# Wide products and transfer-made sums in the first up projection of a decoder trunk, with the down projection's kept sums put earlier

## The chip, the cores and the metric

The kernel runs on one core of a Trainium2 chip. The metric is the time of one execution on the device in microseconds (us); the shown time is the median of three runs. TensorE (PE) multiplies, VectorE (DVE) and ScalarE (ACT) work on tiles, GpSimd (POOL) and SyncE (SP) issue transfers. Transfers that SP or ACT issue go through the hardware queues q1 and q10, those that POOL issues through the software queue q0. All of them are carried by the same 16 DMA engines.

## The reference

One layer over 512 positions of width 1024: two half-weighted SwiGLU blocks around a token mixer, then a last norm. Everything is float32.

```python
def swiglu(x, w_gate, w_up, w_down):
    return (jax.nn.silu(x @ w_gate) * (x @ w_up)) @ w_down
...
        x = x + 0.5 * swiglu(rmsnorm(x, ffn1_norm[l]), ffn1_wg[l], ffn1_wu[l], ffn1_wd[l])
        x = x + hybrid_mixer(rmsnorm(x, mix_norm[l]), w_in[l], conv_w[l], conv_b[l],
...
        x = x + 0.5 * swiglu(rmsnorm(x, ffn2_norm[l]), ffn2_wg[l], ffn2_wu[l], ffn2_wd[l])
    return rmsnorm(x, final_norm)
```

The change touches the first SwiGLU only: its up projection (`w_gate` and `w_up` together, 2816 columns each, 22 tiles of 128 for gate and for up) and the sums of blocks of `w_down` that its down projection will use.

## The kernel before

**Precision.** Every product of two float32 matrices is made of three matmuls on pairs of a high part h and a rest l: h times yh, l times yh, h times yl. ACT copies a weight tile to its high part (`wh`), and DVE subtracts (`wl`).

**The start.** SP issues the eight tiles of x (256 KB each) mixed with three weight tiles in chunks of 128 KB (`wr`), then four more weight tiles of 512 KB (`ahead`), all on q1; ACT issues three small transfers on q10. PE multiplies the three weight tiles as the x tiles come. The first of the four `ahead` tiles (`AH[0]`) is split by `given` (ACT `wh<-ahead`, DVE `wl<-ahead`) and gives the fourth product, `gemm(pu, w, y, range(KD))`.

**The plain tiles.** `ffn_up` begins with eight plain ("direct") tiles of 24 matmuls of 512 columns, in the loop over `d`. At this time SP has no more than the next raw tiles to load.

**The stream.** Then come 16 units w of a block scheme, seven block products each where plain multiplication has eight; per unit the order is 1, 2, 4 (of the unit before), 6, 3 (of the unit before), 5, 7. Product p of unit w multiplies a sum of weight blocks by a sum of activation blocks: s1, s3 are formed by POOL transfers with accumulation into SBUF, s2 = s1 + a11 and s4 = s2 + a12 by DVE in `add_weights`. A narrow product has 12 matmuls of 256 columns into one half of a PSUM tile. A wide one has 4 of 512 columns (h with both halves of the moving operand, into both halves of the tile) and 4 of 256 columns, and its two halves are then added by DVE. Products 2, 5 and 3 are wide (`WIDE`). `step(i)` emits, behind product i, the reading of product i-1 (`results`) and the preparation of the weights of product i+4 (`prepare`). An activation function put into the list `functions` is emitted one step later.

**The down projection's sums.** `block_down` keeps a table of tasks. Task number n is emitted when `ahead(i - len(stream))` reaches n, so with 112 products in the stream, task -90 comes in step 22. For each of eight column blocks j, a sum `kept` in DRAM is made by two POOL transfers of 256 KB: a plain one DRAM to DRAM (task 5j - 90, line 891) and an accumulating one (task 5j - 83, line 892). They are read only in the down projection (`fetch_sum`).

**Order.** Inside `tc.manual_schedule(engines=ENGINES)` the order on each engine is the order of the code. An instruction waits for the semaphores of what it needs. POOL has nothing but its transfers here.

Of the kernel before, what the change touches and what calls it, by code (L numbers as in the profile page):

```python
# [176 lines left out]
def hybrid_kernel(ctx, tc, xt, vec, w1u, w1d, wm, wki, wrg, watt, wrnn, wout, w2u, w2d, gf, out):  # L177
# [224 lines left out]
    class W:  # L402
        pass

    WIDE = (2, 5, 3)

    def weight_blocks(wu, n0, first):

# [7 lines left out]
    def ffn_up(y, wu, n0, hs, g, waiting=(), given=(), ahead=None, blocks={}, wide=()):  # L416
# [10 lines left out]
        ws = [W() for _ in range(count)]  # L427
        for w, o in enumerate(ws):
            o.j, o.blocks = w % 2, blocks.get(w)
            o.wide = range(1, 8) if o.blocks else wide  # L430
        loaded, pairs = [0], {}

        direct = [(n, j) for n in range(n0, f0) for j in range(2)]
# [39 lines left out]
        def load():  # L473

            w = loaded[0]
            loaded[0] += 1
            o = ws[w]
            n = f0 + w // 2 * 2
            u, v = wu[n, o.j], wu[n + 1, o.j]
            if blocks and w + 2 >= min(blocks):  # L480
                o.x = slot(F32, "a11"), slot(F32, "a12")
                for b in range(2):
                    Q.dma_start(o.x[b], u[:, b * H:(b + 1) * H])
            else:
                x_ = raw.tile([P, WMAX], F32, tag="raw", name=nm("wr"))
                o.x = x_[:, :H], x_[:, H:]
                Q.dma_start(x_, u)
            o.s1, o.s3, o.a22 = (slot(F32, t) for t in ("s1", "s3", "a22"))
            Q.dma_start(o.s1, v[:, :H])
            Q.dma_start(o.s3, v[:, :H])  # L490
            Q.dma_start(o.a22, v[:, H:])
            yield
            G.dma_start(o.s1, v[:, H:], accum_op=ALU.add)
            G.dma_start(o.s3, u[:, :H], accum_op=ALU.add)
# [9 lines left out]
        def add_weights(i):  # L504
            p, w = stream[i] if i < len(stream) else (0, 0)
            o = ws[w]
            if o.blocks:
                return
            if p == 6:
                o.s2 = slot(F32, "s2")  # L510
                V.tensor_add(o.s2, o.s1, o.x[0])
            if p == 3:
                o.s4 = slot(F32, "s4")
                V.tensor_add(o.s4, o.s2, o.x[1])

# [13 lines left out]
        def prepare(i):  # L529
            if i < LEAD:  # L530
                add_weights(i)
            if i + 1 >= LEAD:
                add_weights(i + 1)
            p, w = stream[i]
            o = ws[w]
            even = i // 2 * 2
            if i % 2 == 0:
                units.append([wsp.tile([P, WMAX], F32R, tag=t, name=nm(t)) for t in ("wh", "wl")])
            if formed(even) and formed(even + 1):
                if i % 2 == 0:  # L540
                    wsplit(pairs.pop(i // 2), *units[-1])
                    fetch_pair(i + 2 * RAWS)
                return
            h, l = (t[:, i % 2 * H:(i % 2 + 1) * H] for t in units[i // 2])
            if formed(i):
                wsplit(pairs[i // 2][:, i % 2 * H:(i % 2 + 1) * H], h, l)
            else:
                wsplit({1: lambda: o.x[0], 2: lambda: o.x[1], 6: lambda: o.s2, 5: lambda: o.s1, 7: lambda: o.s3,
                        4: lambda: o.a22, 3: lambda: o.s4}[p](), h, l)
            if i % 2:  # L550
                fetch_pair(even + 2 * RAWS)

# [24 lines left out]

        def function(t, o):
            if o.wide:
                functions.append(t)  # L580
            else:
                A.activation(t, t, AF.Silu)

# [3 lines left out]
        def results(p, o, first):  # L587
            if p == 1:
                o.t1, o.t2 = (work("tg"), work("tg")) if o.j == 0 else (awork("tu"), awork("tu"))
                A.activation(o.t1[:, lo], o.beta[:, lo], AF.Copy)  # L590
            elif p == 2:
                V.tensor_sub(o.t1[:, lo], o.p2[:, lo], o.t1[:, lo])
                if p in o.wide:
                    V.tensor_add(o.t1[:, lo], o.t1[:, lo], o.p2[:, hi])
            elif p == 6:
                A.activation(o.t1[:, hi], o.beta[:, lo], AF.Copy)
            elif p == 7:
                A.activation(o.t2[:, hi], o.beta[:, lo], AF.Copy)
                V.tensor_add(o.t2[:, hi], o.gamma[:, lo], o.t2[:, hi])
                if 5 in o.wide:  # L600
                    V.tensor_add(o.t2[:, hi], o.t2[:, hi], o.gamma[:, hi])
                if o.j:
                    o.h2 = slot(F32, "h")
                    V.tensor_mul(o.h2[:, hi], o.t2[:, hi], first.t2[:, hi])
                else:
                    function(o.t2[:, hi], o)
            elif p == 4:
                if o.j:
                    V.tensor_mul(o.h2[:, lo], o.beta[:, lo], first.t2[:, lo])
                else:  # L610
                    A.activation(o.t2[:, lo], o.beta[:, lo], AF.Silu)
            elif p == 3:
                V.scalar_tensor_tensor(o.t1[:, hi], o.gamma[:, lo], -1.0, o.t1[:, hi], op0=ALU.mult, op1=ALU.subtract)
                if p in o.wide:
                    V.tensor_sub(o.t1[:, hi], o.t1[:, hi], o.gamma[:, hi])
                if o.j:
                    o.h1 = slot(F32, "h")
                    V.tensor_mul(o.h1, o.t1, first.t1)
                    hs.extend((o.h1, o.h2))
                else:  # L620
                    function(o.t1, o)
# [43 lines left out]
        def step(i):  # L665


            ready = functions[:]
            functions.clear()
            p, w = stream[i - 1] if i else (0, 0)  # L670
            o, first = ws[w], ws[w - 1]
            if p and o.blocks:
                copies(p, o)
                if p in (2, 3):
                    reads(p, o, first)
            elif p:
                results(p, o, first)
            if i + LEAD < len(stream):
                prepare(i + LEAD)
            if p and o.blocks and p not in (2, 3):  # L680
                reads(p, o, first)
            for t in ready:
                A.activation(t, t, AF.Silu)

        with tc.manual_schedule(engines=ENGINES):
            for _ in range(len(raws), RAWS + len(raws)):
# [2 lines left out]
            operands, norm = moving_operands(g), norm_steps(acc)  # L689
            for d, (n, j) in enumerate(direct):  # L690
                sums.append(psum(("aux", "mm")[n % 2]))
                if d == 1:
                    norm_rest(norm)
                    hs.extend(ffn_act(*p) for p in waiting)
# [58 lines left out]
    def block_down(hs, wd, sums, blocks=None):  # L753
# [100 lines left out]
        for i, st in enumerate(steps):  # L854
# [33 lines left out]
                task(3 * j // 2 + 4, add)  # L888
            if p == 7:
                kept = scr.tile([P, S], F32, name=nm("scr"))  # L890
                task(5 * j - 90, lambda j=j, o=kept: nc.gpsimd.dma_start(o, block(2, j)))
                task(5 * j - 83, lambda j=j, o=kept: nc.gpsimd.dma_start(o, block(0, j), accum_op=ALU.add))

                def fetch_sum(j=j, o=kept):
                    s3[j] = slot(F32, "s3")
# [95 lines left out]

    sums = []
    d1 = block_down(hs, w1d, sums)
    ffn_up(y, w1u, 2, hs, V_G1, ((WP[0], WP[1]), (WP[2], pu)), AH[1:], d1.tasks_at, wide=WIDE)

    BLOCKS2D = down_blocks(w2d)
    BLOCKS2U = weight_blocks(w2u, 0, UNITS)
# [1011 lines left out]
```

## Time and profile before

| | us |
|---|---|
| median of three runs (1065.58 to 1066.42) | 1065.99 |
| the profiled execution | 1064.61 |
| its span, first to last instruction | 1062.8 |
| PE busy | 1052.4 (99%) |
| DVE busy | 881.4 (83%) |
| ACT busy | 667.0 (63%) |
| POOL busy | 235.0 (22%) |

All durations below are from the profiled execution, whose time is 1.8 us over its span and 1.4 us under the median. Times in a timeline count from the start of the span. "PEclk" is the granted clock of TensorE as a share of its higher level, "DMA share" the mean busy share of the 16 DMA engines. A matmul's row gives its own time from first to last column; successive matmuls overlap, so what a product takes is read from start to start.

### The profile page before, as it was taken

The page shows a single profiled execution, that of the slowest core. Times are in us where ns is not written, and L with a number is a line of the kernel's source. Part 1 is how long each engine was busy: PE and PEld are TensorE (multiplying, and loading weights), DVE is VectorE, ACT ScalarE, POOL GpSimd, SP SyncE. Part 2 cuts the span into 40 slices and gives each one's busy share as a digit, 9 for nine tenths or more (in the row PEclk, how much of TensorE's full clock was granted, in tenths as well). Part 3 has the DMA queues.
Part 4 walks back from the last instruction along what each step waited for, and adds up shares of the span by engine and source line. Part 5 has one row for each costly group of instructions (what it writes and reads, how often), then busy time and mean ns, then how long its engine had stood idle before and what let it go on. Part 6 is the DMA issues. An engine that isn't in the chain of part 4 may idle for free.

```text
span 1062.8 us, 16803 instructions
## 1 busy us (share of the span) xinstructions
PE 1052.4 (99%) x5812; PEld 914.6 (86%) x5812; DVE 881.4 (83%) x1730; ACT 667.0 (63%) x1250; POOL 235.0 (22%) x357
## 2 busy tenths in 40 slices
PE   9999999999999999999999999999999999999997
PEld 7889999989999788888888888888899888888885
DVE  6688888889988879998899867766888888888875
ACT  6565656655576657976886664446656666565663
POOL 0161241102131021212031444442643000000020
PEclk9999999999999999999999999999999999999999
DMA  7398899638794487667594878995997666545573
GB/s 279 73 253 203 212 256 235 163 112 247 173 225 120 127 221 183 171 181 184 135 227 129 215 170 201 268 243 151 250 280 182 200 196 194 183 146 170 188 204 121
DMA packets 93973, 203.71 MB, mean 192 GB/s; under 512 B 11712, under 2 KB 20032, under 8 KB 93248
## 3 DMA queue, kind: packets, MB, share of 16 engines
q1 hardware_dynamic: 60144, 136.24, 39.0%
q0 software_dynamic: 33024, 65.55, 31.9%
q8 instruction: 46, 0.75, 0.3%
q10 hardware_dynamic: 720, 0.84, 0.2%
q14 instruction: 39, 0.32, 0.1%
HBM read 191.58 MB, written 48.23 MB: 226 GB/s over the span
## 4 chain that ended last, share of the span: by engine, by line
PE 90%; DVE 6%; ACT 2%; issue 1%; DMA 1%; ACTq 0%; DVEq 0%
PE mm L171 63%; PE aux L171 27%; DVE wl L171 2%; ACT wh L171 1%; DVE am L171 1%; DVE ca L171 1%; ACT cm L171 1%; DMA wr<-wm 0%; DVE xc L171 0%; DVE h L171 0%; DMA vt<-vec 0%; DVE cb L171 0%; DVE tu L171 0%; DVE tg L171 0%; DVE cm L171 0%
## 5 line engine op out<-in xcount | busy, mean ns | idle before, releaser
L171 DVE TENSOR_TENSOR wl<-wr,wh 128x1024 fp32r<-128x1024 f32 (+2 forms) x241 | 237.8, 990 | 72.3 <-ACT wh L171 70.1
L171 ACT ACTIVATE wh<-wr 128x1024 fp32r<-128x1024 f32 (+3 forms) x243 | 208.4, 864 | 75.6 <-issue 23.6
L171 PE MATMUL mm<-cm,wh 128*128 128x256 f32 (+1 forms) x1280 | 250.4, 300 | 0.0
L171 PEld LDWEIGHTS mm<-cm,wh 128*128 128x128 f32 x1280 | 202.8, 191 | 5.1
L171 PE MATMUL mm<-cm,wl 128*128 128x256 f32 x736 | 184.5, 282 | 0.0
L171 PE MATMUL mm<-yh,wh 128*128 128x512 f32 (+1 forms) x416 | 163.7, 394 | 0.4 <-ACT wh L171 0.2
L171 PE MATMUL mm<-yl,wh 128*128 128x512 f32 (+1 forms) x416 | 162.3, 390 | 0.0
L171 PE MATMUL mm<-yh,wl 128*128 128x512 f32 x408 | 159.3, 390 | 0.0
L171 PEld LDWEIGHTS mm<-cm,wl 128*128 128x128 f32 x736 | 133.7, 191 | 4.1
L171 PE MATMUL aux<-cm,wh 128*128 128x512 f32 (+1 forms) x472 | 123.4, 380 | 0.8 <-ACT cm L171 0.5
L171 PEld LDWEIGHTS mm<-yh,wh 128*128 128x128 f32 (+1 forms) x416 | 78.0, 187 | 17.2 <-ACT i L171 0.6
L171 PEld LDWEIGHTS mm<-yl,wh 128*128 128x128 f32 (+1 forms) x416 | 77.6, 187 | 15.6 <-DVE yl L171 0.5
L171 PEld LDWEIGHTS mm<-yh,wl 128*128 128x128 f32 x408 | 76.6, 188 | 16.3
L171 PEld LDWEIGHTS aux<-cm,wh 128*128 128x128 f32 x472 | 79.8, 190 | 10.8 <-ACT cm L171 0.9
L171 ACT ACTIVATE wh<-s 128x512 fp32r<-128x512 f32 x96 | 59.8, 626 | 41.9 <-DVE s L171 38.4
L171 PEld LDWEIGHTS aux<-cm,wl 128*128 128x128 f32 x440 | 68.7, 189 | 8.6
L171 PE MATMUL aux<-cm,wl 128*128 128x256 f32 x440 | 73.9, 281 | 0.0
L171 DVE TENSOR_TENSOR wl<-s,wh 128x512 fp32r<-128x512 f32 x96 | 64.8, 686 | 5.4 <-ACT wh L171 5.3
L325 POOL DMA_DIRECT2D scr<-w2d x32 | 29.8, 1050 | 174.7 <-DMA scr<-w2d 149.3
L159 POOL DMA_DIRECT2D cm<-h x16 | 13.7, 865 | 205.8 <-ACT cm L171 197.1
L171 PE MATMUL mm<-wh,cm 128*128 128x512 f32 x192 | 59.1, 389 | 0.0
L1010 POOL COPY beat<-beat 128x1 f32<-128x1 f32 x67 | 25.0, 373 | 126.7 <-DVE beat L1009 117.1
(263 smaller groups left out, 2138.3 us busy)
## 6 DMA issues: line engine op xcount, KB each, us to landing
wr<-scr SPq DMA_DIRECT2D x80, 256.0 KB, 3.0
wr<-wm SPq DMA_DIRECT2D x39, 512.0 KB, 4.3
scr<-w2u POOLq DMA_DIRECT2D x72, 256.0 KB, 5.7
wr<-w1u SPq DMA_DIRECT2D x21, 512.0 KB, 5.1
scr<-scr POOLq DMA_DIRECT2D x40, 256.0 KB, 5.3
wr<-w1d SPq DMA_DIRECT2D x18, 512.0 KB, 4.4
wr<-w2u SPq DMA_DIRECT2D x36, 256.0 KB, 3.0
wr<-w2d SPq DMA_DIRECT2D x36, 256.0 KB, 3.0
```

The source lines that it names most:

```text
L159: return self.engine.dma_start(out, src, **kw)
L171: return call(*args, **kw)
L325: plain, adds = nc.gpsimd.dma_start, lambda o, i: nc.gpsimd.dma_start(o, i, accum_op=ALU.add)
L1010: nc.gpsimd.tensor_copy(paces[-1], paces[-1])
```

## The change

It has three parts.

1. **Width.** In the first up projection, units 4 to 15 get `WIDE1`, so products 1 and 6 are wide as well. For product 1, ACT copies 512 instead of 256 columns to a tile `c`, DVE subtracts over 512 columns and `joined` adds the halves. For product 6, ACT copies the upper half out of PSUM, DVE adds the lower half to it in PSUM (`o.beta[:, lo]`), and ACT copies the sum out again; in units 4 to 14 that last copy goes through `functions`, one step later.
2. **s4.** In these 12 units s4 is made by an accumulating POOL transfer of a12 (256 KB from DRAM) into the tile of s2, behind the splitting of s2.
3. **Kept sums.** The 16 transfers of the eight kept sums move to tasks j//4 - 200 and j//4 - 199, and the loop over the plain tiles calls `ahead(d - 200)`.

```diff
-    WIDE = (2, 5, 3)
+    WIDE, WIDE1 = (2, 5, 3), (1, 2, 6, 5, 3)
...
-            o.wide = range(1, 8) if o.blocks else wide
+            o.wide = range(1, 8) if o.blocks else wide if w >= 4 or not wide else WIDE
...
-            if p == 3:
+            if p == 3 and 6 not in o.wide:
                 o.s4 = slot(F32, "s4")
                 V.tensor_add(o.s4, o.s2, o.x[1])
...
+            if p == 6 and 6 in o.wide and not o.blocks:
+                o.s4 = o.s2
+                G.dma_start(o.s4, o.a12, accum_op=ALU.add)
...
-                A.activation(o.t1[:, lo], o.beta[:, lo], AF.Copy)
+                if p in o.wide:
+                    o.c = slot(F32, "c")
+                    A.activation(o.c, o.beta, AF.Copy)
+                else:
+                    A.activation(o.t1[:, lo], o.beta[:, lo], AF.Copy)
             elif p == 2:
+                if 1 in o.wide:
+                    V.tensor_sub(o.c, o.p2, o.c)
+                    joined(o.t1[:, lo], o.c)
+                    return
...
             elif p == 6:
-                A.activation(o.t1[:, hi], o.beta[:, lo], AF.Copy)
+                if p in o.wide:
+                    A.activation(o.t1[:, hi], o.beta[:, hi], AF.Copy)
+                    V.tensor_add(o.beta[:, lo], o.beta[:, lo], o.t1[:, hi])
+                if p in o.wide and o is not ws[0] and o is not ws[-1]:
+                    functions.append((o.t1[:, hi], o.beta[:, lo], AF.Copy))
+                else:
+                    A.activation(o.t1[:, hi], o.beta[:, lo], AF.Copy)
...
                 sums.append(psum(("aux", "mm")[n % 2]))
+                if ahead:
+                    ahead(d - 200)
...
-                task(5 * j - 90, lambda j=j, o=kept: nc.gpsimd.dma_start(o, block(2, j)))
-                task(5 * j - 83, lambda j=j, o=kept: nc.gpsimd.dma_start(o, block(0, j), accum_op=ALU.add))
+                task(j // 4 - 200, lambda j=j, o=kept: nc.gpsimd.dma_start(o, block(2, j)))
+                task(j // 4 - 199, lambda j=j, o=kept: nc.gpsimd.dma_start(o, block(0, j), accum_op=ALU.add))
...
-    ffn_up(y, w1u, 2, hs, V_G1, ((WP[0], WP[1]), (WP[2], pu)), AH[1:], d1.tasks_at, wide=WIDE)
+    ffn_up(y, w1u, 2, hs, V_G1, ((WP[0], WP[1]), (WP[2], pu)), AH[1:], d1.tasks_at, wide=WIDE1)
```

On POOL, at the beginning of the program before the change (`ident` is the identity matrix of the setup, `cm` the activation sums of the stream):

```order
masks.py:197 MEMSET ident 128x128
masks.py:199 ISA
masks.py:199 AFFINE_SELECT ident<-ident 128x128
L159 DMA cm_475<-cb_478 128x256
L159 DMA cm_475<-ca_477 128x256
L159 DMA cm_476<-ca_477 128x256
```

and with the change (`scr` are the kept sums; L911 is the plain transfer, L912 the accumulating one):

```order
masks.py:197 MEMSET ident 128x128
L911 DMA scr_339<-w1d 128x512
masks.py:199 ISA
masks.py:199 AFFINE_SELECT ident<-ident 128x128
L911 DMA scr_340<-w1d 128x512
L911 DMA scr_341<-w1d 128x512
L911 DMA scr_342<-w1d 128x512
L912 DMA scr_339<-w1d 128x512
L912 DMA scr_340<-w1d 128x512
L912 DMA scr_341<-w1d 128x512
L912 DMA scr_342<-w1d 128x512
L911 DMA scr_343<-w1d 128x512
```

All 16 transfers now stand ahead of the first `cm` transfer, the first of them ahead of the end of the setup. The plain ones of line 911 wait for nothing, an accumulating one only for the landing of the plain one of its own tile; no instruction of the plain tiles is waited for.

On ACT, from the reading of product 1 to product 7 of one even unit before the change (`mm` is the PSUM tile `beta`, `tg` the tile t1 or t2, `wh` a high part):

```order
L171 ACTIVATE tg_1832<-mm_1796 128x256
L171 ACTIVATE wh_1814<-s_268_1613 128x512
L171 ACTIVATE wh_1851<-s_269_1614 128x512
L171 ACTIVATE wh_1851<-wr_1740 128x512
L171 ACTIVATE tg_1832<-mm_1796 128x256
L171 ACTIVATE wh_1888<-wr_1740 128x512
L171 ACTIVATE wh_1888<-a_270_1615 128x512
L171 ACTIVATE wh_1926<-s_315_1907 128x512
```

and the same stretch with the change:

```order
L171 ACTIVATE c_1810<-mm_1777 128x512
L171 ACTIVATE wh_1791<-s_269_1603 128x512
L171 ACTIVATE wh_1828<-s_270_1604 128x512
L171 ACTIVATE wh_1828<-wr_1721 128x512
L171 ACTIVATE tg_1808<-mm_1777 128x256
L171 ACTIVATE wh_1861<-wr_1721 128x512
L171 ACTIVATE wh_1861<-a_271_1605 128x512
L171 ACTIVATE tg_1808<-mm_1777 128x256
L171 ACTIVATE wh_1897<-s_316_1880 128x512
```

The first copy is twice as wide, and a second copy `tg<-mm` has come in behind two splittings. Product 7 of the unit, which writes the lower half of the same `mm` tile again, waits for it. On DVE the addition in PSUM that this copy waits for stands between two subtractions for weights:

```order
L171 TENSOR_TENSOR wl_1829<-s_270_1604,wh_1828 128x512
L171 TENSOR_TENSOR h_1789<-mm_1660,tg_1567 128x256
L171 TENSOR_TENSOR wl_1829<-wr_1721,wh_1828 128x512
L171 TENSOR_TENSOR mm_1777<-mm_1777,tg_1808 128x256
L171 TENSOR_TENSOR wl_1862<-wr_1721,wh_1861 128x512
```

The fourth row is the new one; before the change the third was followed by the fifth.

## Rows read from the trace of the kernel before

**Rows 1.** The page's first part: busy us, share of the span, instructions.

```profile
PE 1052.4 (99%) x5812; PEld 914.6 (86%) x5812; DVE 881.4 (83%) x1730; ACT 667.0 (63%) x1250; POOL 235.0 (22%) x357
```

**Rows 2.** What PE waits for, longest: total us, times, longest us.

```profile
PE aux L171 <- DVE epst L171: 1.1, 1, 1.1
PE aux L171 <- DVE e L171: 0.5, 1, 0.5
```

**Rows 3.** Timeline of PE, a wide and a narrow product: start, us, operation, tiles, shape.

```profile
77.23 1.09 PE L171 MATMUL aux<-cm,wh 128*128 128x512 f32 x4
...
78.63 0.40 PE L171 MATMUL mm<-cm,wh 128*128 128x256 f32 x2
...
80.07 0.40 PE L171 MATMUL mm<-cm,wh 128*128 128x256 f32 x2
```

**Rows 4.** The first FFN's stream and the whole, groups by shape: busy us, mean ns.

```profile
L171 DVE TENSOR_TENSOR s<-s,wr 128x512 f32<-128x512 f32 x30 | 20.5, 684 | 0.0
L171 DVE TENSOR_TENSOR tg<-aux,tg 128x256 f32<-128x256 f32 x16 | 6.7, 417 | 0.0
L171 DVE TENSOR_TENSOR c<-aux,c 128x512 f32<-128x512 f32 x24 | 16.4, 683 | 0.0
L171 ACT ACTIVATE c<-mm 128x512 f32<-128x512 f32 x24 | 14.2, 595 | 11.7 <-PE mm L171 11.7
```

**Rows 5.** Timelines of ACT, DVE and PE, product 6 to product 7 of a unit.

```profile
135.78 0.38 ACT L171 ACTIVATE tg<-mm 128x256 f32<-128x256 f32 x1 [2.14 <-PE mm L171]
...
136.58 0.62 ACT L171 ACTIVATE wh<-a 128x512 fp32r<-128x512 f32 x1
...
136.71 0.69 DVE L171 TENSOR_TENSOR wl<-wr,wh 128x512 fp32r<-128x512 f32 x1 [0.69 <-ACT wh L171]
...
138.39 0.40 PE L171 MATMUL mm<-cm,wh 128*128 128x256 f32 x2
```

**Rows 6.** Transfers issued in 98 to 163: count, KB each, us to landing.

```profile
scr<-w1d POOLq DMA_DIRECT2D x16, 256.0 KB, 8.1
```

**Rows 7.** Stretches: us, busy PE PEld DVE ACT POOL, PEclk, DMA share, GB/s.

```profile
10.00:15.00 5.00, 5.00 (x24) 4.13 (x23) 4.52 (x9) 5.00 (x12) 0.00 (x0) 1.00 0.97 320
...
25.00:40.00 15.00, 15.00 (x74) 12.57 (x73) 7.17 (x11) 6.70 (x8) 0.00 (x0) 1.00 0.00 1
72.00:222.00 150.00, 149.52 (x1080) 141.19 (x1079) 132.93 (x258) 88.47 (x184) 37.55 (x47) 1.00 0.83 203
```

**Rows 8.** Transfers in 2.6 to 17.2, all on hardware queues.

```profile
DMA packets 3259, 4.77 MB, mean 326 GB/s; under 512 B 468, under 2 KB 2004, under 8 KB 3259
```

**Rows 9.** Queues in 112.2:117.4, 122.9:132 and 142.8:150.2: packets, MB, share of 16 engines.

```profile
q0 software_dynamic: 284, 0.62, 53.2%
q1 hardware_dynamic: 338, 0.89, 48.3%
...
q0 software_dynamic: 410, 0.97, 46.3%
q1 hardware_dynamic: 586, 1.38, 45.6%
...
q0 software_dynamic: 438, 0.90, 55.9%
q1 hardware_dynamic: 556, 1.28, 45.8%
```

**Rows 10.** From AH[0]'s load, issued at 10.79, to its product: DMA issues, ACT, DVE, PE.

```profile
ahead<-w1u SPq DMA_DIRECT2D x1, 512.0 KB, 6.4
...
19.05 1.06 ACT L171 ACTIVATE wh<-ahead 128x1024 fp32r<-128x1024 f32 x1 [2.60 <-PE mm L171]
...
20.14 1.23 DVE L171 TENSOR_TENSOR wl<-ahead,wh 128x1024 fp32r<-128x1024 f32 x1 [2.49 <-ACT wh L171]
...
21.57 0.39 PE L171 MATMUL mm<-yh,wl 128*128 128x512 f32 x1
```

**Rows 11.** Timeline of POOL, 0 to 50: its first transfer.

```profile
46.31 1.03 POOL L159 DMA_DIRECT2D cm<-cb  x1 [45.01 <-DVE cm L171]
```

More of the change, by code (lines that the diff above doesn't have):

```diff
@@ L479, in load @@
             u, v = wu[n, o.j], wu[n + 1, o.j]
+            o.a12 = u[:, H:]
             if blocks and w + 2 >= min(blocks):
@@ L579, in function @@
             if o.wide:
-                functions.append(t)
+                functions.append((t, t, AF.Silu))
             else:
@@ L682, in step @@
             for t in ready:
-                A.activation(t, t, AF.Silu)
+                A.activation(*t)
         with tc.manual_schedule(engines=ENGINES):
```

## The prediction

> **What bounds the kernel now.** I read the engine totals first. PE is busy 1052.4 of a span of 1062.8 us, DVE 881.4, ACT 667.0, POOL 235.0 [rows 1]. So the time is PE's work, and the first question to each edit is whether it takes work from PE or makes it wait. The list of what PE waits for comes next: its longest entry is 1.1 us once, at the very start, and the next is 0.5 us once [rows 2]. Hence almost nothing is to be won by removing waits, and whatever stall a change brings in comes on top, because PE has no idle time further on in which to catch up.
>
> Third, the stretches by engine and DMA share [rows 7]. The change puts transfers from the stream (72 to 222) to another place, so I look at both places. In the stream PE is busy 149.52 of 150 us although the DMA engines are 0.83 busy: the transfers there cost PE nothing. From 10 to 15 us the DMA engines are 0.97 busy: the load of x and of the first weights takes all they have. From 25 to 40 us, under the plain tiles, they stand at 0.00. PEclk is 1.00 in all of these stretches.
>
> **The change part by part.**
>
> *Width.* PE's own gain is the difference between a narrow and a wide product. In the timeline the wide one starts at 77.23 and the next at 78.63, so 1.40 us; that narrow one lasts until 80.07, so 1.44 us [rows 3]. Two products in each of 12 units become wide: 24 x 0.04 = 1.0 us less. On DVE, per unit, product 1 changes two operations of 256 columns to one of 512 and one of 256: 683 + 417 - 2 x 417 = 0.27 us more. Product 6 brings one addition of 0.42 us, and the sum s4 (684 ns) is taken away [rows 4]; 0.27 + 0.42 - 0.68 is zero. ACT has 595 in place of 380 ns for product 1 [rows 4, 5] and one more copy of 0.38, so 0.6 us per unit and 7 us in all; it is busy 88.47 of 150 us there [rows 7], which covers this.
>
> *The late copy.* Product 7 overwrites the half of PSUM that the deferred copy reads, so a new wait of PE appears. In a unit of before, ACT's first copy ends at 135.78 + 0.38 = 136.16; DVE then has an idle gap of 0.69 us just before 136.71 [rows 5], which holds most of the new 0.42 us addition. ACT ends its second splitting at 136.58 + 0.62 = 137.20 and could copy until 137.58. Product 7 starts at 138.39. Slack 0.8 us: I cost the wait at nothing. Queued behind it are all of PE's products; the price if the cover is gone is a rival below.
>
> *s4.* Twelve POOL transfers replace twelve DVE additions. The operand is needed in product 3 of the unit, eight products after product 6: 8 x 1.42 = 11.4 us between the two splittings. The transfers of the same size that stand in this stream land 8.1 us after issue [rows 6]. Some 3 us are left, so nothing; and the stream loses 16 transfers of the same size as it gets 12, so the queues there become no fuller.
>
> *Kept sums.* This decides. The words "under the plain tiles" are not what the order of POOL says: since POOL has nothing else to do and the plain transfers wait for nothing, they are issued as soon as POOL is free, about 1 us after the start of the span (before, POOL has been idle for 45.01 us when its first transfer comes at 46.31, so since 1.30 [rows 11]). There they meet the load of x. From 2.6 to 17.2 us the hardware queues move 4.77 MB at 326 GB/s [rows 8], and the last of it that matters is AH[0], issued at 10.79 and landed 6.4 us later, at 17.2 [rows 10].
>
> What does a pending software queue do to the hardware queue? The start of before has no such case, the stream has: in three stretches where both queues always had work, q1 moved 0.89 MB in 5.2 us, 1.38 in 9.1 and 1.28 in 7.4 [rows 9], so 171, 152 and 173 GB/s, mean 165. Against 326 that is a share of 0.51. The ends are 0.47 and 0.53.
>
> How long is the software queue non-empty? 16 transfers of 0.262 MB are 4.19 MB. In the same three stretches q0 took 4.5, 4.3 and 4.6 us of all 16 engines per MB (53.2% of 5.2 us for 0.62 MB, and so on) [rows 9]; so 18.7 us of all 16 engines, or 37 us at half of them. The additions wait for their plain transfers' landing, but four of each are issued together, so POOL is hardly ever without one under way. The load of 14.6 us of full service thus runs at half service from end to end.
>
> AH[0] then lands at 2.6 + 14.6 / 0.51 = 31.4 instead of 17.2. Behind it come ACT's splitting, 1.06, and DVE's, 1.23; in before, ACT took this tile only at 19.05, since it waited for PE, and the first matmul that needs `wl` started at 21.57 [rows 10]. So there are 21.57 - 17.2 - 2.29 = 2.1 us of cover, and the rest shows: 31.4 + 2.29 - 21.57 = 12.1 us. With the shares 0.53 and 0.47 it is 10.9 and 14.4 us. The stalls before that, where PE waits for late tiles of x, are contained in it, not added: they only spread the same delay. The tiles behind AH[0] come 3.2 us apart at half service (0.524 MB at 165 GB/s) while PE needs at least 15.00 / 74 = 0.20 us for each matmul of a plain tile [rows 7], 4.9 us for the 24 of one; they keep ahead. Nothing later gives the 12 us back: PE is 99% busy from there on.
>
> TensorE's clock is granted in full in these stretches [rows 7], with PE busy nearly throughout; with the change PE would wait for microseconds between tiles of x. The Trainium skill's "TensorE: Matmul & The Clock Gate", Part 1, says that the throttled state is the default and that activity releases it; by that rule some matmuls of the start would run at 1.2 GHz. No run here shows that, and the sum goes without it.
>
> **The sum.** 1064.6 (profiled execution) - 1.0 + 12.1 = 1075.7. The median of the runs shown is 1.4 us above the profiled execution: 1077.1.
>
> **The rivals.**
>
> *Nothing is held up.* The hardware queues keep their service, or the software queue's packets come so slowly at first that the start is loaded before they matter; the 16 transfers then end under the plain tiles, where the engines stand at 0.00. It decides at AH[0] landing before 19.3, that is a hardware share above 14.6 / 16.7 = 0.87. Then only the width is left: 1066.0 - 1.0 = 1065.0, within 0.2% (a measurement of this kernel can tell some 2.1 us from no change). For it: POOL is slow at this, one issue takes it 1.03 us [rows 11]. Against it: no wait holds the transfers in the order of POOL, and no mixed stretch shows a share near 0.87. Faster by over 2.1 us would need, beside the 1.0, that waits of PE outside the start vanish, and the largest of these is 0.5 us once [rows 2].
>
> *The software queue is served first.* If all 18.7 us of its work come before AH[0], it lands at 17.2 + 18.7 = 35.9, and the delay is 35.9 + 2.29 - 21.57 = 16.6 us: 1066.0 - 1.0 + 16.6 = 1081.6. For it: in two of the three stretches q0 took more of the engines than q1 (53.2 and 55.9% [rows 9]), and its packets are larger, 0.90 MB in 438 or 2.1 KB each, against 4.77 MB in 3259 or 1.5 KB at the start [rows 8, 9]. The page "DMA: Bandwidth & Descriptors" of the Trainium skill, section "Queues, rings and completion order", says that each engine goes round robin between its queues, one whole packet from each; by that rule the queue with the bigger packets gets more than half, which is this rival, while the near-even shares of the three stretches agree with a turn for each.
>
> *An operand of the stream comes late.* If the new addition falls behind a 0.69 us subtraction on DVE and the deferred copy behind one more 0.62 us splitting on ACT, the copy ends at about 138.9 instead of 137.58, and product 7 loses 0.5 us in 11 units, 5.7 us; a late s4 would show in the same way. On top of the delay: 1077.1 + 5.7 = 1082.8. Against it are the 0.8 us and the 3 us of slack above.
>
> **How the numbers follow.** Forecast 0.52, at 1077.1 with its own ends 1076 and 1079.4; software queue first 0.20, 1081.6; late operand 0.08, 1082.8; nothing held up 0.20, 1065.0, of which I give 0.04 to faster. So slower 0.80, same 0.16, faster 0.04. The range goes from 1067 to 1084: below it lies most of the last rival, above it little, since the late operand together with the full 16.6 us (1087) or a clock at its lower level would be needed.
>
> **What the profile of the changed kernel would show.** Right: in the stretches from 5 to 30 us, a DMA share near 1 with q0 and q1 about even; POOL issuing from about 1 us on; x's last tiles and AH[0] landing late, AH[0] near 31; PE with waits of about 12 us in all ahead of the `pu` product, mostly for ACT's `yh`, `wh` or the transfers; the same 1.40 us for all wide products; the stream's waits as short as before. Wrong: DMA share of 0.97 until 17 and moved transfers only after; or PE's waits at the start under 2 us. If the waits are there but at product 7 or product 3 of the stream, the late operand was the cause. If they are near 16 us with q0 ahead of q1, the second rival holds.

## The result and the profile after

| | before | after |
|---|---|---|
| median, us | 1065.8 (1065.58 to 1066.42) | 1073.7 (1073.04 to 1074.94) |
| ratio | | 1.0076 (95%: 1.0062 to 1.0089) |
| profiled execution | 1064.61 | 1073.04 |
| its span | 1062.8 | 1071.2 |

The change costs 7.9 us. The forecast was 1077.1 in a range of 1067 to 1084: right in direction and place, 3.4 us too high.

The page after, first part; it answers to [rows 1]. PE's busy time grew by 3.7 us although it has 96 matmuls fewer:

```profile
PE 1056.1 (99%) x5716; PEld 909.7 (85%) x5716; DVE 885.2 (83%) x1730; ACT 672.8 (63%) x1262; POOL 245.3 (23%) x369
```

The best measure of where the time went is the start of one and the same matmul in both timelines. The first matmul of the plain tiles (start us, us, engine, operation), before and after:

```profile
27.23 0.39 PE L171 MATMUL aux<-yh,wh 128*128 128x512 f32 x1
```

```profile
35.29 0.39 PE L171 MATMUL aux<-yh,wh 128*128 128x512 f32 x1
```

So 8.06 us are lost before the first plain tile. Followed further in the same way, the difference stays at 8.06 up to unit 4 of the stream, falls to 7.19 over the 24 products that became wide, rises to 7.41 at product 7 of the last unit, and from 7.42 to 8.33 at the beginning of the second FFN's stream. There it stays to the end; the spans differ by 8.4.

What PE waits for after, the longest (total us, times, longest us), and the rows of the two late steps, product 7 of the last unit and the second FFN's stream (start, us and, in brackets, the idle time before). They answer to [rows 2]:

```profile
PE mm L171 <- ACT wh L171: 2.2, 4, 0.7
PE aux L171 <- DMA cm<-cb: 1.3, 1, 1.3
PE mm L171 <- ACT yh L171: 1.1, 1, 1.1
...
233.93 0.30 PEld L171 LDWEIGHTS mm<-cm,wh 128*128 128x128 f32 x2 [0.16 <-ACT tu L171]
...
774.91 0.47 PE L171 MATMUL aux<-cm,wh 128*128 128x512 f32 x1 [1.26 <-DMA cm<-cb]
```

The stretches of the start after (us, busy PE, PEld, DVE, ACT, POOL, granted clock, DMA share, GB/s), against [rows 7]:

```profile
10.00:15.00 5.00, 4.65 (x19) 2.88 (x18) 2.05 (x5) 2.23 (x5) 3.76 (x6) 1.00 1.11 272
15.00:20.00 5.00, 3.09 (x12) 1.61 (x10) 1.86 (x4) 1.65 (x4) 0.00 (x0) 1.00 1.09 307
20.00:25.00 5.00, 3.84 (x10) 2.44 (x9) 3.06 (x7) 3.77 (x9) 3.34 (x4) 0.68 1.06 392
25.00:30.00 5.00, 5.00 (x23) 4.07 (x22) 3.79 (x6) 3.82 (x7) 0.00 (x0) 0.98 1.08 303
...
35.00:40.00 5.00, 5.00 (x27) 4.29 (x27) 1.40 (x2) 2.61 (x3) 0.00 (x0) 1.00 0.48 195
```

The DMA engines are now full until 35 us, and by 40 nearly done: the transfers are not under the plain tiles but ahead of them. In 10 to 25 PE has 3.4 us without work, and its clock is granted at 0.68 in 20 to 25.

PE's last wait ahead of the plain tiles, and ACT's splitting of `AH[0]`, after; they answer to [rows 10]:

```profile
21.75 0.78 PE L171 MATMUL mm<-yh,wh 128*128 128x512 f32 x1 [1.15 <-ACT yh L171]
...
27.06 1.06 ACT L171 ACTIVATE wh<-ahead 128x1024 fp32r<-128x1024 f32 x1 [1.18 <-PE mm L171]
```

At 21.75 PE has waited for the sixth tile of x. After that it has no wait up to the plain tiles; at 25.25 it is 8.0 us behind the kernel before. `AH[0]` landed at 26.3, but ACT takes it at 27.06 and had waited for PE, not for the landing.

The issue of x's last tile on SP, before and after:

```profile
10.31 0.43 SPq L159 DMA_DIRECT2D x<-xt  x1
```

```profile
15.82 0.33 SPq L159 DMA_DIRECT2D x<-xt  x1
```

So a slow load also starts later. In all fourteen traces of this case SP and POOL issue a transfer only when the eighth before it on the same engine has landed; here that landing came at 15.80.

POOL after (start, us, engine, transfer, idle before); with [rows 11] it shows from when the transfers go, and where POOL waits for their landings:

```profile
1.30 0.69 POOL L911 DMA_DIRECT2D scr<-w1d  x1 [0.36 <-issue]
...
2.32 1.63 POOL L911 DMA_DIRECT2D scr<-w1d  x3
6.04 0.87 POOL L912 DMA_DIRECT2D scr<-w1d  x1 [2.09 <-DMA scr<-w1d]
...
11.29 2.54 POOL L911 DMA_DIRECT2D scr<-w1d  x4
20.11 1.70 POOL L912 DMA_DIRECT2D scr<-w1d  x2 [6.28 <-DMA scr<-w1d]
22.01 1.64 POOL L912 DMA_DIRECT2D scr<-w1d  x2 [0.20 <-issue]
```

The queues after in 13:17, 22:24, 25:31 and 2:24.2, the last being the time until x's last tile landed (packets, MB, share of 16 engines). They answer to [rows 8, 9]:

```profile
q0 software_dynamic: 327, 0.60, 80.8%
q1 hardware_dynamic: 326, 0.35, 31.0%
...
q1 hardware_dynamic: 464, 0.84, 109.0%
q0 software_dynamic: 3, 0.00, 0.1%
...
q0 software_dynamic: 325, 0.60, 54.1%
q1 hardware_dynamic: 329, 1.20, 53.2%
...
q0 software_dynamic: 1216, 3.15, 50.5%
q1 hardware_dynamic: 2684, 3.82, 49.3%
```

Read the packet counts first: 327 against 326, and 325 against 329. While both queues have work, one packet of each goes for one of the other, and the shares follow from how long a packet is: in 13:17 q1's packets hold 1.1 KB and it gets 31%, in 25:31 they hold 3.6 KB and it gets 53%. In 22:24 the software queue is empty and q1 has everything: POOL waited for a landing until 20.11, and the first packets of what it issued then come at 24.2. Over the whole load q1 had 49.3%.

### The profile page after: what moved, and what is told of

The parts are those of the page before. It is cut to its first block, busy times and chain, and to the rows that moved or that the text cites. A ratio compares the mean times of both kernels' runs of the same rounds, so it can differ in the third digit from the quotient of the medians.

```text
span 1071.2 us, 16621 instructions
## 1 busy us (share of the span) xinstructions
PE 1056.1 (99%) x5716; PEld 909.7 (85%) x5716; DVE 885.2 (83%) x1730; ACT 672.8 (63%) x1262; POOL 245.3 (23%) x369
## 4 chain that ended last, share of the span: by engine, by line
PE 89%; DVE 4%; DMA 3%; ACT 3%; issue 1%; SPq 0%; ACTq 0%; POOLq 0%
PE mm L171 63%; PE aux L171 26%; DVE wl L171 1%; DMA wr<-w1u 1%; DMA x<-xt 1%; ACT wh L171 1%; DMA cm<-cb 1%; DVE ca L171 1%; ACT cm L171 1%; DVE h L171 0%; DVE cb L171 0%; ACT L171 0%; DVE tu L171 0%; DVE cm L171 0%; DVE tg L171 0%
## 5 line engine op out<-in xcount | busy, mean ns | idle before, releaser
L171 PE MATMUL mm<-cm,wh 128*128 128x256 f32 (+1 forms) x1184 | 241.2, 310 | 0.0
L171 PEld LDWEIGHTS mm<-cm,wh 128*128 128x128 f32 x1184 | 189.3, 191 | 7.4 <-ACT tu L171 0.2
L171 PE MATMUL mm<-cm,wl 128*128 128x256 f32 x736 | 172.5, 282 | 0.0
L171 PEld LDWEIGHTS mm<-cm,wl 128*128 128x128 f32 x736 | 129.9, 190 | 6.1
L325 POOL DMA_DIRECT2D scr<-w2d x32 | 29.4, 1039 | 174.6 <-DMA scr<-w2d 160.5
L159 POOL DMA_DIRECT2D s<-w1u x44 | 40.6, 1186 | 109.5 <-DVE wl L171 67.0
```

The source lines that it names most:

```text
L159: return self.engine.dma_start(out, src, **kw)
L171: return call(*args, **kw)
L325: plain, adds = nc.gpsimd.dma_start, lambda o, i: nc.gpsimd.dma_start(o, i, accum_op=ALU.add)
```

## The experiments

Positions are those of the first matmul of the plain tiles (27.23 before, 35.29 with the change), from one profile each; times with a ratio are medians beside runs of the kernel before on the same chip.

| run | what it is | plain tiles from | median | ratio (95%) |
|---|---|---|---|---|
| e1 | kept sums early, nothing else | 35.52 | 1074.0 | 1.0078 (1.0063 to 1.0092) |
| e2 | wide products and s4 transfers, sums in the stream | 27.47 | 1068.1 | 1.0019 (1.0010 to 1.0028) |
| e3 | the change, sums held until 25 us | 27.73 | 1068.6 | 1.0025 (1.0015 to 1.0035) |
| e4 | e2 with s4 on DVE | 27.43 | 1065.3 | 0.9995 (0.9986 to 1.0004) |
| e5 | the change, eight more early transfers | 42.84 | 1079.7 (one run) | |
| e6 | the change, only the plain transfers early | 31.35 | 1069.1 (one run) | |
| e7 | the change, sums in pairs with rows of 4 KB | 34.29 | 1071.1 (one run) | |
| e8 | the change, PE kept busy in the start | 35.05 | 1074.5 (one run) | |
| e9 | the change with s4 on DVE | 34.93 | 1072.8 | 1.0063 (1.0048 to 1.0078) |
| e10 | e4, last unit narrow | 27.64 | 1065.5 | 0.9994 (0.9985 to 1.0003) |
| e11 | e4, twelve memsets on POOL | 27.91 | 1065.6 (one run) | |
| e12 | e3 with s4 on DVE | 29.72 | 1067.4 | 1.0014 (1.0004 to 1.0025) |

### Which part costs: the sums alone, the width alone

The kernel before, with the sums alone moved:

```diff
-                task(5 * j - 90, lambda j=j, o=kept: nc.gpsimd.dma_start(o, block(2, j)))
-                task(5 * j - 83, lambda j=j, o=kept: nc.gpsimd.dma_start(o, block(0, j), accum_op=ALU.add))
+                task(j // 4 - 200, lambda j=j, o=kept: nc.gpsimd.dma_start(o, block(2, j)))
+                task(j // 4 - 199, lambda j=j, o=kept: nc.gpsimd.dma_start(o, block(0, j), accum_op=ALU.add))
```

> The kernel before, with the 16 transfers of the kept sums alone put to tasks j//4 - 200 and j//4 - 199 (and the call of ahead in the loop over the plain tiles); no product becomes wide, s4 stays on DVE. Theory A, the moved transfers delay the load of x and of the first weights: the first matmul of the plain tiles, at 27.2 us in the kernel before and at 35.3 with the whole change, starts at 35.3 here as well, and the time is 8.1 us over the kernel before, about 1073.9, that is 0.9 us over the time with the whole change less what a late wait costs. Theory B, the wide products bring in the loss: the plain tiles start at 27 to 28 us and the time stays within 1 us of 1065.8.

Measured: 1074.0, and the plain tiles start at 35.52. Theory A holds; the sums' place alone makes the whole loss, 8.0 us of the median.

The change with those two lines as before:

> The whole change but with the kept sums' transfers back at tasks 5j - 90 and 5j - 83. Theory A: the plain tiles start at 27.2 us as in the kernel before, and 24 products save 0.036 us each less some 0.2 us that the last unit loses at product 7, so 0.7 us under the kernel before: about 1065.1, ratio 0.9993, hardly told from 1. Theory B: 1073 or so, with waits of PE in the stream at products 7 or 3.

Measured: the start is as before (27.47), but 1068.1 instead of 1065.1. B is out, and A missed 3 us. The trace has two late copies at product 7 that the change's own trace does not have (weight loads of PE: start, us, idle before):

```profile
158.90 0.30 PEld L171 LDWEIGHTS mm<-cm,wh 128*128 128x128 f32 x2 [0.27 <-ACT tg L171]
179.18 0.30 PEld L171 LDWEIGHTS mm<-cm,wh 128*128 128x128 f32 x2 [0.34 <-ACT tg L171]
```

and the transfers into s tiles issued on POOL in 140 to 225 land late (first fence: this run, second: the change, third: s4 on DVE, fewer since the s4 transfers are missing; count, KB, median us to landing). For this run and the change the second row has SP's transfers into s tiles, on the hardware queue:

```profile
s<-w1u POOLq DMA_DIRECT2D x23, 256.0 KB, 10.0
...
s<-w1u SPq DMA_DIRECT2D x12, 256.0 KB, 9.4
```

```profile
s<-w1u POOLq DMA_DIRECT2D x24, 256.0 KB, 7.2
...
s<-w1u SPq DMA_DIRECT2D x12, 256.0 KB, 4.5
```

```profile
s<-w1u POOLq DMA_DIRECT2D x15, 256.0 KB, 5.4
```

With the sums and the s4 transfers both in the stream, the DMA engines are 0.92 busy in 72 to 222 (0.82 in the run with s4 on DVE), and transfers come late on both kinds of queue. Six us ahead of the second late copy ACT waits for an s tile:

```profile
172.89 0.63 ACT L171 ACTIVATE wh<-s 128x512 fp32r<-128x512 f32 x1 [1.87 <-DMA s<-w1u]
```

DVE's work behind it slips, and the put-off copy with it. That is the rival of the prediction in which an operand of the stream comes late, in a kernel without the early sums. Together with the wait at the second FFN (below) this profile is 1.3 us of span behind the one with s4 on DVE; the medians differ by 2.9. The profile is of one of the two fastest executions (1066.83); where the others lose the rest is not shown.

### s4 without transfers

```diff
-            if p == 3 and 6 not in o.wide:
+            if p == 3:
                 o.s4 = slot(F32, "s4")
...
-            if p == 6 and 6 in o.wide and not o.blocks:
-                o.s4 = o.s2
-                G.dma_start(o.s4, o.a12, accum_op=ALU.add)
```

> Wide products as in the run with the width alone (kept sums at their old tasks), but s4 is formed by DVE in units 4 to 15 too, without the 12 transfers. DVE then has 0.27 + 0.42 us per unit more than in the kernel before, 8.2 us in 12 units, of 150 us of which 133 are busy. Theory A, DVE is not what PE waits for: the time is that of the width alone within 0.3 us, 1065.1. Rival, the transfers are needed because DVE falls behind: PE waits for DVE in the stream, 2 to 8 us more.

Measured: 1065.3, ratio 0.9995. DVE bears the 8 us more (busy 889.7 us against 881.4). The 12 transfers bought nothing here and cost 2.9 us.

The same edit made to the whole change:

> The whole change with s4 formed by DVE in all units, without the 12 transfers; the kept sums stay early. The width alone with s4 by transfers ran at 1068.1, with s4 on DVE at 1065.3, and the traces of all three kernels with these transfers show a wait of PE of some 0.9 us for a transfer at the start of the second FFN's stream that the kernels without them do not show. Theory A, the s4 transfers cost wherever they are: plain tiles start at 35.3 us as with the whole change, the wait at 766 to 775 us is under 0.5, and the time is 1 to 3 us under that of the whole change, 1071 to 1073. Rival, they only cost where they share the stream with the kept sums' transfers: 1073.7 as with the whole change.

Measured: 1072.8, within theory A's 1071 to 1073, but only 0.9 us under the change where it had 1 to 3; the intervals of the two ratios overlap. The wait for a transfer at the second FFN's beginning is gone from the trace. A gap on POOL goes with it, in the first group of transfers of that stream: with the s4 transfers (first fence, from the run with the width alone) the third one comes 2.3 us after the second, without them (second fence, e4) 0.8 us. The transfers behind it are issued hardly later, but land later: the `cb` that PE waits for landed 30.4 us after the group's first issue in the change and 29.3 in e9.

```profile
738.49 1.18 POOL L159 DMA_DIRECT2D cm<-ca  x1
740.75 0.86 POOL L159 DMA_DIRECT2D cm<-ca  x1 [1.08 <-ACT wh L171]
```

```profile
737.90 2.07 POOL L159 DMA_DIRECT2D cm<-ca  x2
```

To see whether the number of POOL instructions ahead of it decides, twelve memsets of one column took the transfers' places (against e4):

```diff
+            if p == 6 and 6 in o.wide and not o.blocks:
+                G.memset(beat[:, :1], 0.0)
```

> The wide products with s4 on DVE, and in place of each of the 12 s4 transfers POOL does one memset of one column that nothing needs. Question: why do the three kernels with s4 transfers issue the third transfer of the second FFN's first group 2.4 us later than the two without, with the same engines and the same waits around it. Theory 1, the number of instructions on POOL ahead of it (12 more) decides, as in the fetching of POOL's instructions: the wait of PE at 766 us of some 0.9 us is there again. Theory 2, it is the transfers themselves (their number in the queue, or the semaphores that they take in turn): no wait over 0.4 us there.

Measured: no such gap on POOL and no wait there, so it is not the count of instructions, as theory 1 had it. But theory 2 as I put it falls too when all thirteen kernels are laid side by side. The gap is there in the five in which the program has 12 software transfers more than before (the change, e2, e3, e6, e8) and in none of those with as many as before (e1, e4, e9 to e12), with 4 more (e7) or with 20 more (e5), though e5 and e7 have the s4 transfers. The turns of eight in which POOL waits for landings would treat 4, 12 and 20 alike. What is left is the place that this one transfer has in the count of all of them; the mechanism is open. Nor does the wait follow from the gap alone: in e8 PE waited only 0.19 us there. So the wait goes with this count and not with s4 as such, as far as these runs show.

### Under the plain tiles in earnest

```diff
+                    if d == 0:
+                        G.tensor_copy(beat[:, :1], raws[len(given) + RAWS - 1][:, :1])
                     ahead(d - 200)
```

> The whole change, and POOL first copies one column of the third raw weight tile of the plain tiles (landed at 25.4 us in the kernel before) before it issues the 16 transfers, so that they really lie under the plain tiles. Theory A: 18.7 us of DMA work fall into a stretch in which the DMA engines stood at 0.00; the start is as in the kernel before, the plain tiles start at 27.2 us, and the time is 1065.1, as with the wide products alone. If the transfers' tail still delays the stream's first loads from 45 us on, the stream shows a new wait of up to 2 us. Theory B: as with the whole change, 1073.7.

Measured: the start is as before (27.73), yet 1068.6. The chain of landings is longer than the plain tiles: the last held transfer, issued at 42.56, landed at 52.99, the stream's first activation transfers behind it in the same queue landed late, and PE waited at the stream's beginning (two waits in all, one of them that of the second FFN):

```profile
PE aux L171 <- DMA cm<-cb: 3.4, 2, 2.1
```

With s4 on DVE as well:

> The kept sums' transfers held until the third raw weight tile has landed, as in the run that ended at 1068.6, but s4 on DVE, without the 12 transfers. In that run the held transfers ended at 53 us and PE waited 2.1 us for a transfer at the start of the stream, 1.5 us more than with the kept sums in the stream. Theory A, s4's transfers cost 2 to 3 us here too, and the held transfers 1.5: 1065.5 to 1067. Rival, holding alone makes the 1068.6: over 1068.

Measured: 1067.4, between the two theories. By the medians s4's transfers cost 1.2 us in this setting, which is not clear of noise (the intervals of e3 and e12 overlap), and holding the sums 2.1 against e4. This run's own profile was its slowest execution, and had lost 2.5 us by the time of 11 us, before any held transfer was issued:

```profile
8.20 0.63 PE L171 MATMUL mm<-yh,wh 128*128 128x512 f32 x1
8.63 0.63 PE L171 MATMUL mm<-yl,wh 128*128 128x512 f32 x1
```

From 5.4 to 10.3 us its matmuls start 0.43 us apart, where the kernel before has 0.23, as at half the clock, although the view gives the clock as 1.00 there; what caused it is open. So I take only the median. A position of the plain tiles from one profile should be trusted to half a microsecond at best: without early sums it was 27.2 to 27.9 in six kernels, and 29.7 here. Of three places, start, plain tiles and stream, the stream, where they were, is the cheapest for the kept sums.

### What the start's delay is made of

Eight more plain transfers among the second four (on POOL two stand behind each of the four):

```diff
+                for _ in range(2 * (j > 3)):
+                    spare = scr.tile([P, S], F32, name=nm("scr"))
+                    task(-199, lambda j=j, o=spare: nc.gpsimd.dma_start(o, block(2, j)))
```

> The whole change, with eight more plain transfers of 256 KB (copies into spare tiles that nobody reads) queued on POOL behind the second four plain ones. With the whole change the plain tiles' first matmul starts at 35.3 us (27.2 before), and between 22 and 24 us the software queue stands empty, since POOL waits for landings; there the hardware queue gets all engines and the last tiles of x and AH[0] catch up. Theory A, each hardware packet waits for one software packet as long as that queue is not empty: without the gap the tiles of x and AH[0] come 3 to 5 us later, and the plain tiles start at 38 to 40 us. Rival, the delay is a fixed price of having the transfers early (POOL's work, the first landings): they start at 35.3 us.

Measured: the plain tiles start at 42.84, 7.5 us after those of the change where theory A had 3 to 5; the direction is its, the size nearly double. The delay is not a fixed price. Nor did these plain transfers wait for nothing: POOL issued the fourteenth at 15.58 after waiting 1.22 us for an earlier landing, the sixth's, and so on with the eighth before each. The stretches show what filling the gap did: PE nearly idle in 25 to 30, and the clock at half in 30 to 35:

```profile
25.00:30.00 5.00, 0.86 (x3) 0.38 (x3) 0.73 (x2) 0.71 (x2) 1.19 (x2) 0.86 0.97 276
30.00:35.00 5.00, 2.80 (x6) 1.91 (x7) 2.47 (x4) 2.79 (x5) 0.81 (x1) 0.50 1.05 358
```

The plain transfers alone early:

> The whole change, with only the eight plain transfers of the kept sums early and the eight accumulating ones back at tasks 5j - 83. The plain ones take some 5.3 us of all 16 engines (512 packets of 165 ns), the accumulating ones 11.8. Theory A, the load of the start is delayed by the software queue's work served before it: at most 5.3 us, of which some 3 us are covered, so the plain tiles start at 29.5 to 31 us, not at 35.3. Rival, the early transfers cost by their number or by POOL's issue: half of them, half the delay, 31.3 us or more.

Measured: 31.35, a delay of 4.12. That is outside what theory A gave and on the rival's number: half the transfers, half the delay. A's cover of 3 us, that of AH[0], was the wrong one: the 4.1 us are lost by 17 us, in waits like this one for chunks of the weights (`wh`) and in one for a tile of x, before AH[0] is needed:

```profile
12.68 0.50 PE L171 MATMUL mm<-yh,wh 128*128 128x512 f32 x1 [0.84 <-ACT wh L171]
```

The same bytes in half the transfers, with longer packets:

```diff
+                if j % 2 == 0:
+                    pair = scr.tile([P, 2 * S + 16], F32, name=nm("scr"))[:, :2 * S]
+                    row = lambda b, j=j: wd[b * (PAIRS // 2) + j // 2]
+                    task(j // 4 - 200, lambda o=pair, r=row: nc.gpsimd.dma_start(o, r(2)))
+                    task(j // 4 - 199, lambda o=pair, r=row: nc.gpsimd.dma_start(o, r(0), accum_op=ALU.add))
+                kept = pair[:, j % 2 * S:(j % 2 + 1) * S]
```

> The whole change, with the kept sums made in pairs: four plain and four accumulating transfers of 512 KB with rows of 4 KB in place of eight and eight of 256 KB with rows of 2 KB; the same bytes at the same place. Theory A, the engines take turns by packet: a longer software packet takes more of the engines, x's sixth tile lands 1 to 3 us later than the 20.96 us with the whole change, and the plain tiles start at 36.5 to 38.5 us. Rival, the two queues share the engines' time evenly whatever their packets: 35.3 us, within 0.5.

Measured: 34.29, neither of the two. The rule of turns is there, with q1 pressed further down than with the change in the same stretch 13:17:

```profile
q0 software_dynamic: 211, 0.74, 85.8%
q1 hardware_dynamic: 223, 0.21, 18.8%
```

But x's sixth tile landed at 20.44, not later than 20.96: the software queue with its longer packets is through its work sooner and then waits longer for landings (8.43 us against 6.28):

```profile
19.88 0.83 POOL L914 DMA_DIRECT2D scr<-w1d  x1 [8.43 <-DMA scr<-w1d]
```

And half the number of transfers did not halve the delay (7.06 against 8.06), so e6's number was not the number's doing.

What remains is the software work that is served before x's last tile has landed. The rows of the queue, from 2 us to that landing, of e6, e7 and e5 (the change's row is above):

```profile
q0 software_dynamic: 640, 2.10, 34.0%
```

```profile
q0 software_dynamic: 864, 3.15, 49.2%
```

```profile
q0 software_dynamic: 1784, 5.04, 59.2%
```

| | x's last tile landed | later than before (14.64) | q0 until then, us of all engines |
|---|---|---|---|
| e6 | 19.04 | 4.4 | 0.340 x 17.0 = 5.8 |
| e7 | 23.47 | 8.8 | 0.492 x 21.4 = 10.5 |
| the change | 24.27 | 9.6 | 0.505 x 22.2 = 11.2 |
| e5 | 31.40 | 16.8 | 0.592 x 29.4 = 17.4 |

The tile is late by the software work served ahead of it less some 0.6 to 1.7 us, in all four, whatever the number and the size of the packets. Since the engines are full until then and q1 has about the same to move (3.7 to 4.1 MB), this is near to an account of the engines' time. It measures how late the load is, not what PE waits for: in e6 PE had lost its 4.1 us before this tile landed.

### The clock in the start

```diff
             for i in range(3 if k < KD - CH else 0):
+                for _ in range({(4, 0): 2, (4, 1): 3, (4, 2): 3, (5, 0): 5}.get((k, i), 0)):
+                    T.matmul(idle_ps[:, :P], mean, mean, start=True, stop=True)
                 mm3(WP[i], WS[i][1:], slice(k * P, (k + 1) * P), y[k], k == 0, False)
```

> The whole change, with 13 small matmuls into an unused PSUM tile put ahead of products of the start for which PE waits for tiles of x and of the weights (2, 3 and 3 ahead of the fifth tile's three products, 5 ahead of the sixth tile's first), so that PE is busy where it stood idle. With the whole change the granted clock was 0.68 in 20 to 25 us, and eight matmuls from 21.75 on took 1.7 us more than at the full clock. Theory A: the granted clock stays at 1.00, and the plain tiles start at 33.6 us, 1.7 earlier than with the whole change, at 35.3. Rival, the wait for the data alone sets the start and the clock's loss is caught up by it: 35.3 us.

Measured: the clock stayed at 1.00 in every stretch, and the plain tiles start at 35.05, 0.24 us earlier, which is within what one profile can tell. The rival holds: at the full clock PE only waits longer for x's last tile (0.51 us for `yl` at 26.30). The run with the sums alone (e1) says the same without spare matmuls: its clock did not fall either, and its plain tiles start at 35.52. The stretch 20 to 25 of e8 and of e1, against the change's 0.68:

```profile
20.00:25.00 5.00, 4.71 (x25) 3.55 (x23) 3.13 (x7) 3.78 (x8) 3.16 (x4) 1.00 1.06 386
```

```profile
20.00:25.00 5.00, 3.25 (x12) 2.15 (x13) 3.02 (x6) 4.13 (x9) 3.35 (x4) 1.00 1.05 410
```

### A version to keep

> The wide products with s4 on DVE and the kept sums at their old tasks (1065.3, ratio 0.9995), and the last unit of the stream keeps the narrow products 1 and 6. In the traces the last unit lost 0.2 to 0.5 us at product 7, since its copy out of PSUM is not put off. Theory: this wait goes, against 0.07 us of PE's work that comes back, so 0.1 to 0.4 us less, 1065.0, ratio 0.999; if it is as before within 0.3 us, nothing of the width can be measured.

Measured: 1065.5, ratio 0.9994, not to be told from e4 or from the kernel before, although in the trace the last unit's wait is gone. The width is worth what its product shows, 0.87 us, and that is inside the scatter (the 25 runs of the kernel before beside e1 to e4 lie between 1064.27 and 1068.19).

## Why the prediction was right, and where it was not

**Width, 1.0 us:** right. In the change's timeline the two wide products follow each other at 118.01, 119.41 and 120.82, 1.40 and 1.41 us, as [rows 3] had it, and 24 of them brought 0.87.

**The late copy, nothing:** right for the eleven units whose copy is put off; the last unit, whose copy is not, lost 0.22. The prediction did not look at that unit.

**s4, nothing:** right in the first stream, where the cover held, with landings of 7.2 us against [rows 6]. The 0.9 us that the change's timeline loses at the second FFN's first transfers, 500 us further on, are gone without the 12 transfers (e9); no view of the kernel before could have shown them. The sentence that the queues become no fuller, since 16 transfers go and 12 come, held only as long as the 16 did go: with both in the stream (e2) the same edit cost 2.9.

**Kept sums, 12.1 us:** the mechanism is right and shown (e1), the size was 8.1. Of the steps: the transfers were issued from 1.30 us on, as said. The share of 0.51 was right as a mean, 49.3% of the engines until x's last tile. "POOL is hardly ever without one under way" failed: POOL waited 6.28 us for the second four plain transfers, the queue ran dry in 22 to 24, and AH[0] landed at 26.3 (issued 17.52, 8.8 us) instead of 31.4. Filling that gap took the delay to 15.6 (e5). And "the stalls before that are contained in it" failed with it: put into the prediction's own formula, the measured landing gives 26.3 + 2.29 - 21.57 = 7.0 us, less than the 8.1 that were lost. The path through AH[0] did not set the start; chunks of the weights and tiles of x came late before it, and PE had no wait after 21.75. So the half share was right and the path on which the delay was priced was not; that the size came as near as it did is in part luck.

**The rivals.** *Nothing held up* is out, as q1 had 0.49 and not 0.87 of the engines. *The software queue first*, 16.6 us, did not come: its four last transfers were issued from 20.11 us on, too late for the start. But its reason, more than half for the queue with the longer packets, was there in 13:17, with 80.8% against 31.0%, at 327 packets against 326. The Trainium skill says in "DMA: Bandwidth & Descriptors", section "Queues, rings and completion order", that an engine goes round robin between its queues a packet at a time; the trace agrees. The prediction weighed the near-even shares of [rows 9] against it; those were stretches in which both queues had packets of 2 KB and more. Nor did both queues "always" have work there: in the third, q1 starts no packet until 144. Where both had work, the kernel before shows the same counts already (144.4:148):

```profile
q0 software_dynamic: 221, 0.52, 56.8%
q1 hardware_dynamic: 222, 0.68, 49.7%
```

*An operand of the stream comes late* did not happen in the change and did in e2 (its price of 5.7 us is 11 x 0.5, so 5.5).

**The clock:** the change was granted 0.68 in 20 to 25 us after 1.91 us of idle time in 15 to 20; e1, with 1.39 us of idle time there, kept 1.00. The Trainium skill's "TensorE: Matmul & The Clock Gate", Part 1, has the throttled state as the default, released by activity; the change's trace agrees. The sum was right to leave it out, since the plain tiles start within 0.24 us of the change's in both runs that kept the full clock (e1, e8).

## What to carry to other kernels

A transfer that waits for nothing starts when its engine reaches it, not where the code that emits it stands: read its place from the engine's order, and hold it by what it should wait for. If it meets a load that PE waits for, that load comes late by about the time that the engines spend on the transfer before it is through. Read shares from packets, in slices in which both queues have some, and not from bytes over a long stretch. And the DMA engines are a resource: work that is moved to an idle engine's transfers comes late if they are already busy, so weigh it against the sums on the engine that had them.

## What was not expected of the hardware

- The two kinds of queue went packet for packet (327 against 326, 325 against 329, 211 against 223, before the change 221 against 222), so a queue with packets of 1 KB had 19 to 31% of the engines and one with 3.6 KB 53%.
- With twelve more software transfers in the program, one transfer of the second FFN was issued 2.3 us after its neighbour, in five kernels of five; with none, four or twenty more, or twelve memsets, 0.8 us. The cause is open.
- POOL and SP each had at most eight transfers under way: the next was issued only when the eighth before it had landed, in all fourteen traces.
- Keeping PE busy through its waits held the granted clock at 1.00 (e8, against 0.68) and brought 0.24 us, no more than one profile can tell.
